# RWKV block: closing products grouped by array tile, Gram products of the two heads in turn, last doubling level in 64x64 tiles, gates on all rows

## The chip, the cores and the metric

The kernel runs on one core of a Trainium2 chip. The core has a matrix engine (PE, with a weight-load side, PEld), three engines for elementwise work (DVE, ACT, POOL), a queue engine for transfers (SP), and 16 DMA engines. The metric is the device time of one execution in microseconds; less is better. A time is the median of several runs. A profile is one further execution, recorded instruction by instruction; its times are counted from the start of its span.

## What is computed

One layer of a streaming encoder for two groups of tokens, 2048 of a prompt and 32 of a sample, with shared weights: a modulated RMSNorm, one input projection into three groups of heads (RWKV-7 time mixing, attention with forgetting, HGRN2), an output projection, then a SwiGLU network. The change is in the RWKV-7 part, which the reference writes as a scan over tokens:

```python
def rwkv7_mix(p, prev, S0, mu, w0, w2, a0, a2, g2, k_k, k_a, r_k, ln_w, ln_b):
    ...
    r, k, v, wl, al, gl = jnp.split(xs, RW_SPLITS, axis=-1)
    w_raw = -jax.nn.softplus(-(w0 + jnp.tanh(wl) @ w2)) - 0.5
    w = jnp.exp(-jnp.exp(w_raw))
    a = jax.nn.sigmoid(a0 + al @ a2)
    g = jax.nn.sigmoid(gl) @ g2
    ...
    def step(S, inp):
        r_t, k_t, v_t, kk_t, a_t, w_t = inp
        s_kk = jnp.einsum('bhvk,bhk->bhv', S, kk_t)
        S = (S * w_t[:, :, None, :] - s_kk[..., None] * (kk_t * a_t)[:, :, None, :]
             + v_t[..., None] * k_t[:, :, None, :])
        return S, jnp.einsum('bhvk,bhk->bhv', S, r_t)
    ...
    mean = jnp.mean(y, axis=-1, keepdims=True)
    var = jnp.mean(jnp.square(y - mean), axis=-1, keepdims=True)
    y = ((y - mean) * lax.rsqrt(var + RW_GN_EPS)).reshape(B, T, RW_WIDTH) * ln_w + ln_b
    bonus = jnp.sum(r * k * r_k, axis=-1, keepdims=True) * v
    y = (y + bonus.reshape(B, T, RW_WIDTH)) * g
    return y, S_T
```

There are four RWKV heads of 64 channels. The three small factors wl, al and gl have 32, 32 and 64 channels.

## The kernel before

The program first projects and recurs (`project_and_recur`), then runs attention, the output projection and the feed-forward part (`rest`). In the first part `interleave` takes turns among generators: the input projection of the next 512 tokens (lines 360 to 362, tile `ip_p`, products on the full array), the RWKV blocks, the HGRN2 blocks (tiles `hg_...`) and side work. A scheduler then orders the instructions of each engine once and for all; each engine works through its own queue in that order, with semaphores between them.

`rwkv_block` works on 128 tokens, two chunks of 64, of one pair of heads; channels of the pair lie on partitions 0 to 63 and 64 to 127 (the slices `hs`). There are 32 such blocks for the prompt and two of one chunk for the sample. Each step of a block ends in a `yield`. Its products go to one of three PSUM buffers (`rw_ps`), and ACT or DVE takes them out. The steps that matter here:

- **gates** (line 1091): three products of the low-rank factors `rl_e` (32, 32 and 64 partitions of one tile) with the weights `lw` in the same partitions. The first stands in a step of its own, the other two in one step.
- **Gram products** (line 1155): per head and chunk, `rw_kb` (lines 1143 and 1147) with `rw_G`, 64 rows by 128 columns, masked by DVE (line 1159); the second head comes a step later. POOL then scales `rw_kb` in place (line 1167), and PE transposes it (line 1170).
- **doubling**: the inverse of a unit triangular 64x64 matrix (`rw_tt`, transpose `rw_tn`), doubled from blocks of 2 to 32. Levels 2 to 16 are a loop, two products each (lines 1204 and 1213, 64x64 tiles, 32 columns moving), with an ACT copy and a masked DVE copy. The level 32 stands alone (lines 1226 and 1233), in 32x32 tiles, with two copies of 32 partitions on each engine.
- **states** (line 1268): a small chain from chunk to chunk.
- **closing products** (lines 1279 and 1280): per chunk and head two products that add up in the same 64 columns of a PSUM buffer: one with all 128 rows (128x64), one with 64 (64x64).
- **normalisation** (lines 1286 to 1300): means over the 64 channels of a head are products with constant matrices, `bmean` (ones over 64) and `rkb` (ones scaled by a weight). HGRN2 uses `bmean` too.

The closing products as they stand:

```python
        for i, h in enumerate(hs):
            nc.tensor.matmul(ps[h, cc], lhsT=wu[:, i, c, 1, :], rhs=gm[i][:, c, 64:128], start=True, stop=False)
            nc.tensor.matmul(ps[h, cc], lhsT=states[c][h, :], rhs=rp_[h, c, 0, :], start=False, stop=True)
```

## Time and profile before

| | us |
|---|---|
| median of 3 runs (3729.07 to 3733.69) | 3733.6 |
| the profiled execution | 3737.9 |
| its span, first to last instruction | 3736.2 |
| PE busy in the span | 3558.0 |
| DVE, ACT, POOL busy | 1925.2, 1501.1, 1382.6 |
| granted PE clock over the span, as a share of full speed | 0.968 |

The page counts an instruction as busy from its start to its end. Matmuls are pipelined: several are under way at once, and one that starts while the last still runs costs only the distance between the two starts. So the timeline is read from start to start. Its rows give start and length in us, engine, line, operation, output and inputs by the program's names, the part of the array (rows\*columns), the moving operand (partitions x elements), and how many instructions of a kind stand in a row. A float32 product shows as two passes, one of the projection (float32 in a rounded form) as one.

### The profile page before, as it was taken

The page shows a single profiled execution, that of the slowest core. Times are in us where ns is not written, and L with a number is a line of the kernel's source. Part 1 is how long each engine was busy: PE and PEld are TensorE (multiplying, and loading weights), DVE is VectorE, ACT ScalarE, POOL GpSimd, SP SyncE. Part 2 cuts the span into 40 slices and gives each one's busy share as a digit, 9 for nine tenths or more (in the row PEclk, how much of TensorE's full clock was granted, in tenths as well). Part 3 has the DMA queues.
Part 4 walks back from the last instruction along what each step waited for, and adds up shares of the span by engine and source line. Part 5 has one row for each costly group of instructions (what it writes and reads, how often), then busy time and mean ns, then how long its engine had stood idle before and what let it go on. Part 6 is the DMA issues. An engine that isn't in the chain of part 4 may idle for free.

```text
span 3736.2 us, 62897 instructions
## 1 busy us (share of the span) xinstructions
PE 3558.0 (95%) x24242; PEld 2969.9 (79%) x24242; DVE 1925.2 (52%) x4482; ACT 1501.1 (40%) x3526; POOL 1382.6 (37%) x1607
## 2 busy tenths in 40 slices
PE   7999999999999998899999999899999999999999
PEld 5888888888778885666666666678999998999998
DVE  3456656566565755656666655642333444333336
ACT  4355556555555645444343443331222213111212
POOL 5334444343343431644443443243233334222323
PEclk9999999999998998999999999999999999999999
DMA  6433333333542245322222213543222223111222
GB/s 216 136 103 101 83 109 120 106 95 98 177 137 73 78 122 159 121 75 74 59 77 65 81 49 75 182 137 96 68 68 74 74 71 123 59 55 56 63 62 93
DMA packets 363648, 361.38 MB, mean 97 GB/s; under 512 B 36511, under 2 KB 305396, under 8 KB 362292
## 3 DMA queue, kind: packets, MB, share of 16 engines
q1 hardware_dynamic: 325216, 320.02, 28.4%
q10 hardware_dynamic: 37748, 37.29, 3.2%
q8 instruction: 191, 3.13, 0.4%
q14 instruction: 109, 0.89, 0.1%
q0 software_dynamic: 384, 0.05, 0.0%
HBM read 291.14 MB, written 66.14 MB: 96 GB/s over the span
## 4 chain that ended last, share of the span: by engine, by line
PE 77%; DVE 6%; POOL 5%; DMA 4%; issue 4%; ACT 3%; ACTq 0%; POOLq 0%; SPq 0%; DVEq 0%
PE ff_p L1834 8%; PE ff_p L1833 8%; PE ff_p L1832 8%; PE ff_o L1783 4%; PE ff_o L1784 4%; PE ff_o L1782 4%; PE ip_p L360 4%; PE ip_p L362 4%; PE ip_p L361 4%; PE pb_pv L690 3%; PE pb_sc L643 2%; PE pb_ps L706 2%; PE pb_ps L707 1%; PE op_p L1692 1%; PE op_p L1691 1%
## 5 line engine op out<-in xcount | busy, mean ns | idle before, releaser
L1834 PE MATMUL ff_p<-h_hi,wil 128*128 128x384 f32 (+2 forms) x1760 | 623.3, 354 | 1.1 <-POOL wil L1719 1.1
L1833 PE MATMUL ff_p<-h_lo,wih 128*128 128x384 f32 (+2 forms) x1760 | 624.2, 355 | 0.1
L1832 PE MATMUL ff_p<-h_hi,wih 128*128 128x384 f32 (+2 forms) x1760 | 622.5, 354 | 1.5 <-DVE op_r L1694 0.4
L1719 POOL TENSOR_TENSOR wil<-ff_st,wih 128x1024 fp32r<-128x1024 f32 x134 | 322.2, 2404 | 582.2 <-ACT wih L1718 551.1
L360 PE MATMUL ip_p<-h_hi,w_hi 128*128 128x256 f32 (+1 forms) x1472 | 452.0, 307 | 14.0 <-ACT h_hi L296 5.9
L361 PE MATMUL ip_p<-h_lo,w_hi 128*128 128x256 f32 (+1 forms) x1472 | 436.7, 297 | 2.7 <-POOL h_lo L297 1.5
L362 PE MATMUL ip_p<-h_hi,w_lo 128*128 128x256 f32 (+1 forms) x1472 | 437.2, 297 | 0.3 <-DVE w_lo L318 0.3
L1832 PEld LDWEIGHTS ff_p<-h_hi,wih 128*128 128x128 f32 x1760 | 332.3, 189 | 17.5 <-DVE ff_sg L1763 0.8
L1834 PEld LDWEIGHTS ff_p<-h_hi,wil 128*128 128x128 f32 x1760 | 333.9, 190 | 14.4 <-POOL wil L1719 1.5
L1833 PEld LDWEIGHTS ff_p<-h_lo,wih 128*128 128x128 f32 x1760 | 332.6, 189 | 14.5 <-POOL h_lo L1907 0.6
L360 PEld LDWEIGHTS ip_p<-h_hi,w_hi 128*128 128x128 f32 x1472 | 291.4, 198 | 29.8 <-ACT h_hi L296 6.3
L1719 POOL TENSOR_TENSOR wol<-ff_st,woh 128x1024 fp32r<-128x1024 f32 x66 | 162.8, 2471 | 405.7 <-ACT woh L1718 405.6
L700 POOL TENSOR_TENSOR fx_acc<-fx_acc,fx_pt 128x512 f32<-128x512 f32 (+3 forms) x176 | 206.6, 1188 | 264.4 <-PE pb_pv L690 154.9
L1841 DVE TENSOR_TENSOR ff_sg<-ff_sg,ff_p 128x384 f32<-128x384 f32 (+2 forms) x110 | 64.5, 587 | 460.2 <-PE ff_p L1834 459.9
L361 PEld LDWEIGHTS ip_p<-h_lo,w_hi 128*128 128x128 f32 x1472 | 290.6, 197 | 9.6 <-issue 2.7
L1788 DVE TENSOR_TENSOR acc<-acc,ff_o 128x512 f32<-128x512 f32 (+1 forms) x306 | 209.1, 685 | 172.8 <-PE ff_o L1784 172.2
L1782 PE MATMUL ff_o<-woh,act_h 128*128 128x512 f32 (+1 forms) x724 | 287.9, 398 | 9.9 <-ACT act_h L1842 7.2
L362 PEld LDWEIGHTS ip_p<-h_hi,w_lo 128*128 128x128 f32 x1472 | 291.0, 198 | 7.1 <-issue 3.7
L1718 ACT ACTIVATE wih<-ff_st 128x1024 fp32r<-128x1024 f32 x134 | 142.0, 1060 | 370.6 <-PE ff_p L1833 310.5
L1783 PE MATMUL ff_o<-wol,act_h 128*128 128x512 f32 (+1 forms) x724 | 288.0, 398 | 0.0
L1784 PE MATMUL ff_o<-woh,act_l 128*128 128x512 f32 (+1 forms) x724 | 288.0, 398 | 0.0
L1718 ACT ACTIVATE woh<-ff_st 128x1024 fp32r<-128x1024 f32 x66 | 69.3, 1058 | 365.9 <-PE ff_o L1784 343.8
(466 smaller groups left out, 7718.7 us busy)
## 6 DMA issues: line engine op xcount, KB each, us to landing
ff_st<-w_ffn_in SPq DMA_DIRECT2D x132, 512.0 KB
w_st<-w_in SPq DMA_DIRECT2D x88, 512.0 KB
ff_st<-w_ffn_out SPq DMA_DIRECT2D x68, 512.0 KB
cm<-ip_e SPq DMA_DIRECT2D x92, 256.0 KB
x_t<-w_ada SPq DMA_DIRECT2D x32, 512.0 KB
fx_kr<-cm SPq DMA_DIRECT2D x80, 128.0 KB
w_st<-w_in SPq DMA_DIRECT2D x16, 520.0 KB
w_a<-w_ada SPq DMA_DIRECT2D x8, 1024.0 KB
```

Source lines behind the costliest of these rows:

```text
L360: nc.tensor.matmul(ps[:, :T], lhsT=whi[:, d, us], rhs=S.hi[:, d, :T], start=(d == 0), stop=False)
L361: nc.tensor.matmul(ps[:, :T], lhsT=whi[:, d, us], rhs=S.lo[:, d, :T], start=False, stop=False)
L362: nc.tensor.matmul(ps[:, :T], lhsT=wlo[:, d, us], rhs=S.hi[:, d, :T], start=False, stop=(d == ND - 1))
L1718: nc.scalar.activation(hi, st, AF.Copy)
L1719: nc.gpsimd.tensor_tensor(lo, st, f32(hi), ALU.subtract)
L1782: nc.tensor.matmul(ps[:m], lhsT=ah[:, js], rhs=wh[:, cs], start=(n == 0), stop=False)
L1783: nc.tensor.matmul(ps[:m], lhsT=ah[:, js], rhs=wl[:, cs], start=False, stop=False)
L1784: nc.tensor.matmul(ps[:m], lhsT=al[:, js], rhs=wh[:, cs], start=False, stop=(n == 1))
L1788: nc.vector.tensor_tensor(acc[j][:m, cs], acc[j][:m, cs], ps[:m], ALU.add)
L1832: nc.tensor.matmul(ps[:, :S], lhsT=w[0][:, ds], rhs=hh[:, d, :S], start=(d == 0), stop=False)
L1833: nc.tensor.matmul(ps[:, :S], lhsT=w[0][:, ds], rhs=hl[:, d, :S], start=False, stop=False)
L1834: nc.tensor.matmul(ps[:, :S], lhsT=w[1][:, ds], rhs=hh[:, d, :S], start=False, stop=(d == ND - 1))
```

## The change

- The closing products of a block are issued in two groups: first all 128x64 ones, then all 64x64 ones. Only the first product starts the sum, and the checks on groups are switched off.
- The Gram products of both heads are issued in one step, heads in turn, into two PSUM buffers.
- The loop of the doubling runs to 32, and the level with 32x32 tiles goes.
- `lw` gets three slices of 128 partitions with zeros outside their rows, cleared by POOL, and each gate multiplies all 128 partitions.
- `bmean` and `rkb` go; `bones` (ones) takes their place, and the factors move into the DVE or ACT instruction behind or ahead of the product.
- The states of a pair have 5 buffers instead of 6.

```diff
-    K.lw = cp.tile([128, 256], F32, name="lw")
-    nc.scalar.dma_start(out=K.lw[0:32, :], in_=a["rw_w2"][0])
-    nc.scalar.dma_start(out=K.lw[32:64, :], in_=a["rw_a2"][0])
-    nc.scalar.dma_start(out=K.lw[64:128, :], in_=a["rw_g2"][0])
+    K.lw = cp.tile([128, 3, 256], F32, name="lw")
+    nc.gpsimd.memset(K.lw, 0.0)
+    nc.scalar.dma_start(out=K.lw[0:32, 0, :], in_=a["rw_w2"][0])
+    nc.scalar.dma_start(out=K.lw[32:64, 1, :], in_=a["rw_a2"][0])
+    nc.scalar.dma_start(out=K.lw[64:128, 2, :], in_=a["rw_g2"][0])
...
-        nc.tensor.matmul(ps[:, :T], lhsT=K.lw[r0:r1, cs], rhs=lora[r0:r1, :], start=True, stop=True)
+        nc.tensor.matmul(ps[:, :T], lhsT=K.lw[:, i, cs], rhs=lora, start=True, stop=True)
...
-    gm = []
-    for h in hs:
-        ps = pt()
-        for c in range(NCH):
+    gm, gps = [], [pt() for _ in hs]
+    for c in range(NCH):
+        for ps, h in zip(gps, hs):
             nc.tensor.matmul(ps[:, 128 * c:128 * c + 128], lhsT=kb[h, c, :, :], rhs=G[h, 0:2, c, :], start=True, stop=True)
+    for ps in gps:
         v = ps[:, :128 * NCH].rearrange("p (c x) -> p c x", x=128)
...
-    for h_ in (2, 4, 8, 16):
+    for h_ in (2, 4, 8, 16, 32):
...
-        nc.vector.transpose(tn, tt)
+        if h_ < 32:
+            nc.vector.transpose(tn, tt)
         yield
-
-    ps = pt()
...
-            nc.tensor.matmul(ps[up[i], 32 * c:32 * c + 32], lhsT=m, rhs=tn[lo[i], c, 0:32], start=True, stop=True)
-    for h in up:
-        nc.scalar.activation(x[h], ps[h, :32 * NCH].rearrange("p (c x) -> p c x", x=32), AF.Copy)
-    yield
...
-            nc.tensor.matmul(ps[lo[i], 32 * c:32 * c + 32], lhsT=x[up[i], c, :], rhs=tt[up[i], c, 32:64], start=True,
-                             stop=True)
-    for h in lo:
-        nc.vector.tensor_copy(tt[h, :, 32:64], ps[h, :32 * NCH].rearrange("p (c x) -> p c x", x=32))
-    yield
...
-        s = rp.tile([128, 64], F32, name=f"rw_s{p}", bufs=6)
+        s = rp.tile([128, 64], F32, name=f"rw_s{p}", bufs=5)
...
     for c in range(NCH):
-        cc = slice(64 * c, 64 * c + 64)
         for i, h in enumerate(hs):
-            nc.tensor.matmul(ps[h, cc], lhsT=wu[:, i, c, 1, :], rhs=gm[i][:, c, 64:128], start=True, stop=False)
-            nc.tensor.matmul(ps[h, cc], lhsT=states[c][h, :], rhs=rp_[h, c, 0, :], start=False, stop=True)
+            nc.tensor.matmul(ps[h, 64 * c:64 * c + 64], lhsT=wu[:, i, c, 1, :], rhs=gm[i][:, c, 64:128], start=(c == 0),
+                             stop=False, skip_group_check=True)
+    for c in range(NCH):
+        for h in hs:
+            nc.tensor.matmul(ps[h, 64 * c:64 * c + 64], lhsT=states[c][h, :], rhs=rp_[h, c, 0, :], start=False, stop=True,
+                             skip_group_check=True)
...
-    nc.tensor.matmul(ps[:, :T], lhsT=K.bmean, rhs=y, start=True, stop=True)
-    nc.vector.tensor_tensor(y, y, ps[:, :T], ALU.subtract)
+    nc.tensor.matmul(ps[:, :T], lhsT=K.bones, rhs=y, start=True, stop=True)
+    nc.vector.scalar_tensor_tensor(y, ps[:, :T], -1.0 / 64, y, ALU.mult, ALU.add)
...
-    nc.tensor.matmul(ps[:, :T], lhsT=K.bmean, rhs=t1, start=True, stop=True)
-    nc.scalar.activation(t1, ps[:, :T], AF.Ln, bias=K.eps_c[:, 1:2])
+    nc.tensor.matmul(ps[:, :T], lhsT=K.bones, rhs=t1, start=True, stop=True)
+    nc.scalar.activation(t1, ps[:, :T], AF.Ln, bias=K.eps_c[:, 1:2], scale=1.0 / 64)
...
-    nc.vector.tensor_tensor(kp, kp, xr, ALU.mult)
+    nc.vector.scalar_tensor_tensor(kp, kp, vec(K, "rw_r_k", p), xr, ALU.mult, ALU.mult)
...
-    nc.tensor.matmul(ps[:, :T], lhsT=K.rkb[:, p, :], rhs=kp, start=True, stop=True)
+    nc.tensor.matmul(ps[:, :T], lhsT=K.bones, rhs=kp, start=True, stop=True)
```

Two places in PE's queue show how the order changes. The first is around the Gram products of a block in the middle of the projection; each row gives line, operation, output and inputs, and size. `ip_p` is the projection, L1300 the last normalisation product of an older block, L1226 the first half of the last doubling level. Before:

```order
L1155 MATMUL rw_ps<-rw_G,rw_kb 128x128 x2
L1300 MATMUL rw_ps<-rw_a,rkb 128x128
L1226 MATMUL rw_ps<-rw_tn,rw_m_12340 32x32
L1226 MATMUL rw_ps<-rw_tn,rw_gm_12362 32x32
L1226 MATMUL rw_ps<-rw_tn,rw_m_12340 32x32
L1226 MATMUL rw_ps<-rw_tn,rw_gm_12362 32x32
L361 MATMUL ip_p<-h_lo,w_hi 128x256
L362 MATMUL ip_p<-h_hi,w_lo 128x256
L360 MATMUL ip_p<-h_hi,w_hi 128x256
L361 MATMUL ip_p<-h_lo,w_hi 128x256
L1155 MATMUL rw_ps<-rw_G,rw_kb 128x128 x2
L362 MATMUL ip_p<-h_hi,w_lo 128x256
```

After (L1151, L1280 and L1201 are the changed kernel's lines for L1155, L1300 and the doubling's first product):

```order
L1151 MATMUL rw_ps<-rw_G,rw_kb 128x128 x4
L1280 MATMUL rw_ps<-rw_a,bones 128x128
L362 MATMUL ip_p<-h_hi,w_lo 128x256
L360 MATMUL ip_p<-h_hi,w_hi 128x256
L361 MATMUL ip_p<-h_lo,w_hi 128x256
L362 MATMUL ip_p<-h_hi,w_lo 128x256
L1201 MATMUL rw_ps<-rw_tn,rw_m_12303 64x32
L1201 MATMUL rw_ps<-rw_tn,rw_gm_12322 64x32
L1201 MATMUL rw_ps<-rw_tn,rw_m_12303 64x32
L1201 MATMUL rw_ps<-rw_tn,rw_gm_12322 64x32
```

The second head's Gram products move up beside the first's, so PE visits their form once; the last doubling level has the lines and sizes of the levels before it and stands four projection passes later.

The second place is the closing products of a block, also in PE's queue; `rw_gm_...` with `rw_wu` are the 128x64 products of the two heads, `rw_rp` with `rw_s_...` the 64x64 ones. Before:

```order
L362 MATMUL ip_p<-h_hi,w_lo 128x256
L1279 MATMUL rw_ps<-rw_gm_12338,rw_wu 64x64
L1280 MATMUL rw_ps<-rw_rp,rw_s_12161 64x64
L1279 MATMUL rw_ps<-rw_gm_12362,rw_wu 64x64
L1280 MATMUL rw_ps<-rw_rp,rw_s_12161 64x64
L1279 MATMUL rw_ps<-rw_gm_12338,rw_wu 64x64
L1280 MATMUL rw_ps<-rw_rp,rw_s_13052 64x64
L1279 MATMUL rw_ps<-rw_gm_12362,rw_wu 64x64
L1280 MATMUL rw_ps<-rw_rp,rw_s_13052 64x64
L1213 MATMUL rw_ps<-rw_tt,rw_x_1460 64x32 x4
```

After, at the same place (L1255 and L1259 are the two groups, L1210 the doubling's second product):

```order
L362 MATMUL ip_p<-h_hi,w_lo 128x256
L1255 MATMUL rw_ps<-rw_gm_12301,rw_wu 64x64
L1255 MATMUL rw_ps<-rw_gm_12322,rw_wu 64x64
L1255 MATMUL rw_ps<-rw_gm_12301,rw_wu 64x64
L1255 MATMUL rw_ps<-rw_gm_12322,rw_wu 64x64
L1259 MATMUL rw_ps<-rw_rp,rw_s_12121 64x64 x2
L1259 MATMUL rw_ps<-rw_rp,rw_s_13008 64x64 x2
L1210 MATMUL rw_ps<-rw_tt,rw_x_1456 64x32 x4
```

The products are the same and stand between the same neighbours; only their order among themselves changes, from eight changes of form to one.

## Prediction

> **What bounds the kernel now.** I read the stretches of the span first, then the waits of the matrix engine (PE) in the one stretch that the change touches, then its timeline there.

> ```profile
> PE 3558.0 (95%) x24242; PEld 2969.9 (79%) x24242; DVE 1925.2 (52%) x4482; ACT 1501.1 (40%) x3526; POOL 1382.6 (37%) x1607
> 0.00:163.00 163.00, 131.35 (x972) 118.75 (x973) 60.86 (x155) 65.63 (x116) 74.52 (x186) 0.96 0.55 182
> 163.00:1361.00 1198.00, 1156.26 (x11686) 986.33 (x11685) 725.86 (x2459) 681.83 (x2154) 463.31 (x896) 0.95 0.36 107
> 1361.00:2460.00 1099.00, 1010.03 (x5167) 713.67 (x5166) 655.98 (x1243) 474.04 (x838) 445.15 (x324) 0.96 0.33 95
> ```

> The first row gives busy time of the engines over the whole span; the others give, for a stretch, its length, then busy time and instructions of PE, PEld (weight loads), DVE, ACT and POOL, the granted clock, the share of the DMA engines and GB/s. I cut the span so that the second stretch, 163 to 1361 us, holds all matrix products of the RWKV blocks. There PE is busy for 1156 of 1198 us, 97%, while DVE has 61%, ACT 57%, POOL 39% and the DMA engines 36%. The stretch is as long as PE needs for the instructions in its queue, plus 42 us of waiting. From the last closing product on, the order of instructions is the same in both kernels on all five engines, so what lies behind only starts earlier. The question is how much PE time goes, and how much of that comes back as waiting.

> ```profile
> PE rw_ps L1155 <- DVE rw_kb L1147: 9.9, 8, 2.6
> PE rw_ps L1170 <- POOL rw_kb L1167: 8.2, 8, 2.4
> PE rw_ps L1204 <- DVE rw_tn L1216: 3.5, 4, 1.1
> ```

> These are the three longest of PE's waits in the stretch (us in total, times, longest one): short ones, each behind a chain of small DVE, ACT or POOL instructions.

> **The change, part by part.** A float32 product shows as two passes, so "x8" below is four products. The form (64\*64, 128\*64, ...) is the part of the array used, rows by columns. What counts is start to start, since the ends overlap. There are 32 prompt blocks (16 pieces of 128 tokens, 2 head pairs) and 2 sample blocks of half the size.

> *Closing products.*

> ```profile
> 604.05 0.33 PE L1279 MATMUL rw_ps<-rw_gm,rw_wu 128*64 128x64 f32 x2
> 604.30 0.32 PE L1280 MATMUL rw_ps<-rw_rp,rw_s 64*64 64x64 f32 x2
> ...
> 606.10 0.39 PE L391 MATMUL ip_p<-w_hi,h_lo 128*128 128x260 f32 x1
> 917.07 0.45 PE L1261 MATMUL rw_ps<-rw_wu,rw_gm 128*64 128x64 f32 x8
> 917.46 0.24 PE L1204 MATMUL rw_ps<-rw_tn,rw_m 64*64 64x32 f32 x1
> 668.47 0.45 PE L1194 MATMUL rw_ps<-rw_wu,rw_gm 64*64 64x64 f32 x8
> 668.85 0.38 PE L361 MATMUL ip_p<-h_lo,w_hi 128*128 128x256 f32 x1
> ```

> Before, the eight products of a block alternate between two forms, and each costs 0.25 us, 2.05 us in all. Afterwards four of form 128\*64 come first, then four of 64\*64. L1261 is the first group exactly (same form, same sizes, heads in turn) and takes 0.39 us; L1194 is the second and takes 0.38 us. So 2.05 - 0.77 = 1.28 us go per block, 41 us for 32; a sample block has half as many, some 0.6 us each. **41 us**, bounds 39 and 43.

> [...]

> *Gram products.*

> ```profile
> 614.97 0.71 PE L1155 MATMUL rw_ps<-rw_G,rw_kb 64*128 64x128 f32 x4
> 615.61 0.49 PE L1300 MATMUL rw_ps<-rw_a,rkb 128*128 128x128 f32 x2
> 498.86 0.48 PE L1155 MATMUL rw_ps<-rw_G,rw_kb 64*128 64x128 f32 x2
> 499.27 0.49 PE L1300 MATMUL rw_ps<-rw_a,rkb 128*128 128x128 f32 x2
> 671.40 0.65 PE L1244 MATMUL rw_ps<-rw_kn,rw_tt 64*64 64x128 f32 x8
> 671.89 0.19 PE L1204 MATMUL rw_ps<-rw_tn,rw_m 64*64 64x32 f32 x1
> ```

> A head's visit to the form 64\*128 takes 0.64 us with four passes and 0.41 with two: 0.115 us a pass and 0.18 for coming and going. Now both heads come in one visit of eight passes, alternating between the upper and the lower rows. No row shows two such tiles at once. If the passes don't overlap, the visit takes 0.18 + 8 x 0.115 = 1.10 and 0.18 us is saved; if pairs run together, it takes 0.64 and 0.64 is saved. L1244 is the nearest: 64\*64 tiles of both heads with the same 128 columns moving, eight passes in 0.49, which only fits pairs. I take pairs: 32 x 0.64 = 20 us, and 2 us for fewer changes from and to the full array (next rows). **22 us**, bounds 8 and 24.

> *Gates.*

> ```profile
> 638.32 0.28 PE L362 MATMUL ip_p<-h_hi,w_lo 128*128 128x256 f32 x1
> 638.44 0.28 PE L360 MATMUL ip_p<-h_hi,w_hi 128*128 128x256 f32 x1
> 638.65 0.42 PE L1213 MATMUL rw_ps<-rw_tt,rw_x 64*64 64x32 f32 x8
> 639.00 0.39 PE L361 MATMUL ip_p<-h_lo,w_hi 128*128 128x256 f32 x1
> 918.17 0.48 PE L1091 MATMUL rw_ps<-rl_e,lw 32*128 32x128 f32 x2
> 918.59 0.33 PE L1268 MATMUL rw_ps<-rw_s,rw_rp 64*64 64x64 f32 x4
> 601.20 0.90 PE L1091 MATMUL rw_ps<-rl_e,lw 32*128 32x128 f32 x4
> 602.03 0.49 PE L1439 MATMUL hg_ps<-hg_x,hg_k 64*64 64x160 f32 x4
> 423.85 0.39 PE L1128 MATMUL rw_ps<-rw_kk,bones 128*128 128x128 f32 x2
> 424.07 0.39 PE L1286 MATMUL rw_ps<-rw_y,bmean 128*128 128x128 f32 x2
> 424.38 0.24 PE L1204 MATMUL rw_ps<-rw_tn,rw_m 64*64 64x32 f32 x1
> ```

> A pass of the projection (L362 to L360) costs 0.12 us, the step from it to another form 0.21. A block's first gate costs 0.42 us, the other two together 0.83. With all rows a gate has the form of L1128, which comes from and goes to the full array in 0.22, and L1286 leaves it in 0.31. Among full-array work the pair falls from 0.83 to 0.53, the single gate from 0.42 to between 0.22 and 0.31, and 0.09 goes at each entry. Between two small forms the change of form is still paid and little is saved. In the order about half of the visits begin beside full-array work: 34 x about 0.38 = **13 us**, bounds 0 (all between small forms) and 24.

> *Last level.*

> ```profile
> 621.04 0.31 PE L1233 MATMUL rw_ps<-rw_tt,rw_x 32*32 32x32 f32 x8
> 621.28 0.39 PE L360 MATMUL ip_p<-h_hi,w_hi 128*128 128x256 f32 x1
> ```

> In 32\*32 tiles a half of the level takes 0.24 us; in 64\*64, as L1213 above, 0.35. Twice 0.11 for 33 blocks' worth is 7 us lost; where the neighbours are 64\*64 too, the changes of form go and nothing is lost. **6 us lost**, bounds 0 and 7. Two half-height copies become one on ACT (L1228) and on DVE (L1236), which lie beside PE's work; without that cover they would be worth some 0.2 us each per block.

> ```profile
> L1228 ACT ACTIVATE rw_x<-rw_ps 32x64 f32<-32x64 f32 x64 | 13.8, 215 | 38.5 <-PE rw_ps L1226 34.2 <-PE rw_ps L1155 1.5 <-POOL rw_y L1304 1.4
> L1236 DVE COPY rw_tt<-rw_ps 32x64 f32<-32x64 f32 x64 | 13.6, 213 | 11.4 <-PE rw_ps L1233 10.6
> 0.96 0.31 POOL L80 MEMSET sc<- 128x256 f32 x1
> 30.64 1.06 ACT L316 ACTIVATE w_hi<-w_st 128x1024 fp32r<-128x1024 f32 x1 [5.92 <-DMA w_st<-w_in]
> ```

> *The rest.* The means by one matrix of ones instead of two scaled ones keep the number and the sizes of the products; the DVE and ACT instructions take a scale and keep their sizes. The new clearing of the gate weights on POOL is three times the memset of L80, 0.9 us as an estimate, ahead of three DMA issues in ACT's queue. ACT sits idle for 5.92 us soon after, until the weights land, which hides it; without that it costs 0.9 us once. Five state buffers instead of six: a block needs three at a time, and the next one brings two, so none is waited for. All of this: 0.

> **Sum.** PE work: -41 - 22 - 13 + 6 = -70 us, 6% of the 1156; by the bounds -39 - 8 - 0 + 7 = -40 and -43 - 24 - 24 + 0 = -91. Not all comes through. The chains behind the 42 us of waits keep their length while the PE work that covers them gets 6% shorter, and chains that just fitted now show. In return POOL's step L1167 may begin once both heads' Gram products are done, which now happens in one visit, so its 8.2 us should shrink. I put the net at 14 us given back, 20% of the 70: **-56 us**. The profiled execution took 3737.9 us (span 3736.2 and 1.7 around it), 0.1% over the median 3733.6; 3737.9 - 56 = 3682 there, **3678** by the median.

> **Rivals.**
> - *The Gram tiles don't pair.* 14 us less PE work, 45 us net: 3689. For it: no row shows two 64\*128 tiles at once. Against: L1244. Chance 0.13.
> - *Waits swallow more.* The block is a long chain, and PE's order is fixed; if half of the 70 returns as waits: 3699, with three quarters 3716. For it: waits on single DVE and POOL instructions of up to 2.6 us. Against: 97% busy. Chance 0.13.
> - *More comes through.* The wait for POOL goes, gates and Gram reach their upper bounds: -80, 3654. Chance 0.14.
> - [...] Chance 0.04.
> - *Slower: the Gram visit takes two of the three PSUM buffers of the block at once*, so both heads wait until two are free and the next product until DVE has masked one. DVE is 61% busy, and the longest wait here was 2.6 us. From 1.7 us per visit on (56 / 33) the gain is gone; at 2.6 us it would be 86 us and the time 3764. Against: the places of the visits in PE's queue hardly move. Chance 0.04.

> **How the numbers follow.** My forecast of 3678, between 3664 and 3690, has 0.52. The range runs from 3650 to 3710: it leaves out the rival that is slower, the far end of the waits and of the upper bounds. 0.2%, 7.5 us, is about what a measurement of this kernel tells from no change. All cases but one end faster by more; with something for a mix of small gains and new waits: faster 0.92, same 0.04, slower 0.04.

> **What would show it.** In the profile of the changed kernel the four products of the first closing group should take 0.39 us and the second 0.38; eight Gram passes 0.64 (1.10 if unpaired); a gate among full-array work 0.22 to 0.31; PE busy in the RWKV stretch about 1085 us, the waits 50 to 60 us, the stretch some 1142 us long, and the stretches behind it as before. I am wrong if the stretch shortens by less than 30 us, or if PE's busy time falls by 70 us and the stretch does not follow.

## The result, and the profile after

| | kernel before | kernel after |
|---|---|---|
| median of the runs | 3731.3 us (3727.5 to 3733.7, 4 runs) | 3646.6 us (3640.3 to 3650.6, 4 runs) |
| ratio, with its 95% interval | | 0.9772 (0.9755 to 0.979) |
| profiled execution | 3737.9 us | 3650.6 us |
| PE busy in the RWKV stretch | 1156 of 1198 us | 1054 of 1111 us |
| waits of PE there | 42 us | 57 us |

The change made the kernel 85 us faster. 56 were forecast, and 3647 lies just outside the range from 3650 to 3710. The next fence has the engines' row of the page after; the second one two stretches, with the columns as above.

```profile
PE 3454.1 (95%) x24242; PEld 2893.4 (79%) x24242; DVE 1917.3 (53%) x4445; ACT 1486.8 (41%) x3492; POOL 1376.2 (38%) x1608
```

```profile
163.00:1274.00 1111.00, 1054.07 (x11709) 914.95 (x11709) 717.62 (x2426) 669.10 (x2124) 460.72 (x900) 0.98 0.39 116
1274.00:2373.00 1099.00, 1009.29 (x5164) 712.82 (x5162) 654.94 (x1242) 473.81 (x838) 444.36 (x324) 0.96 0.33 95
```

Over the whole span PE is busy for 104 us less (3454 against 3558). The first stretch ends where the last RWKV product ends, 87 us earlier than before. The second is 1099 us long, as before. So the whole gain lies in the RWKV stretch, as forecast. PE is busy for 102 us less there, where 70 were forecast, and waits 15 us longer. The granted clock in the row is 0.98; before it was 0.95.

The timeline of PE shows the new groups (start, length, line, form, passes; "..." leaves out what stands between).

```profile
572.22 0.49 PE L1088 MATMUL rw_ps<-rl_e,lw 128*128 128x128 f32 x2
572.46 0.37 PE L389 MATMUL ip_p<-w_hi,h_hi 128*128 128x260 f32 x1
...
576.52 0.61 PE L1088 MATMUL rw_ps<-rl_e,lw 128*128 128x128 f32 x4
577.06 0.62 PE L1419 MATMUL hg_ps<-hg_x,hg_k 64*64 64x160 f32 x6
...
578.87 0.28 PE L390 MATMUL ip_p<-w_lo,h_hi 128*128 128x260 f32 x1
579.08 0.45 PE L1255 MATMUL rw_ps<-rw_gm,rw_wu 128*64 128x64 f32 x8
579.46 0.45 PE L1259 MATMUL rw_ps<-rw_rp,rw_s 64*64 64x64 f32 x8
579.84 0.39 PE L391 MATMUL ip_p<-w_hi,h_lo 128*128 128x260 f32 x1
...
589.17 0.72 PE L1151 MATMUL rw_ps<-rw_G,rw_kb 64*128 64x128 f32 x8
589.82 0.54 PE L1419 MATMUL hg_ps<-hg_x 64*64 64x96 f32 x6
```

Start to start, the closing groups take 0.38 and 0.38 us (0.39 and 0.38 forecast, 2.05 before); with the entry from the product ahead, eight changes of form have become two, not one. Eight Gram passes take 0.65 us (0.64 forecast; 1.10 if the tiles did not pair). Here a single gate takes 0.24 (0.22 to 0.31 forecast among full-array work; over all single visits the median is 0.32) and a pair 0.54 (0.53). The prices in the prediction came out. The waits of PE in the stretch, the longest five:

```profile
PE rw_ps L1210 <- ACT rw_x L1205: 9.6, 16, 1.5
PE rw_ps L1201 <- DVE rw_tn L1214: 8.9, 13, 1.1
PE rw_ps L1151 <- DVE rw_kb L1144: 7.3, 6, 2.3
PE rw_ps L1221 <- DVE rw_tt L993: 4.4, 4, 2.4
PE rw_ps L1229 <- ACT rw_wu L1224: 4.3, 4, 3.2
```

The wait for POOL's L1167 (8.2 us before) is gone. In its place the two products of a doubling level (L1201, L1210) wait for the DVE and ACT steps between them: the chains that just fitted now show.

**Where the other 30 us are.** The granted clock has two values in the traces of both kernels, 1.00 and 0.50, here called full and half. Before, 123 us of the stretch ran at half clock, after 44 us (the mean of 0.95 over 1198 us says the same: 2 x 0.05 x 1198 = 120). PE's time therefore has three parts. I put every step from one pass to the next at the mean that steps between the same two shapes have at full clock: their sum is the *work*. What the steps during half clock took beyond that is *lost to half clock*. The rest, in which PE stands idle, is *waits*. For the first pair of profiles this gives work 1103 to 1034 us, lost to half clock 53 to 19, waits 42 to 57: -68 - 34 + 15 = -87. The terms of the prediction, -70 and +14, came out near; it had no term for the clock.

### The profile page after: what moved, and what is told of

The parts are those of the page before. It is cut to its first block, busy times and chain, and to the rows that moved or that the text cites. A ratio compares the mean times of both kernels' runs of the same rounds, so it can differ in the third digit from the quotient of the medians.

```text
span 3648.6 us, 62814 instructions
## 1 busy us (share of the span) xinstructions
PE 3454.1 (95%) x24242; PEld 2893.4 (79%) x24242; DVE 1917.3 (53%) x4445; ACT 1486.8 (41%) x3492; POOL 1376.2 (38%) x1608
## 4 chain that ended last, share of the span: by engine, by line
PE 72%; DVE 7%; POOL 6%; ACT 6%; DMA 5%; issue 4%; ACTq 0%; SPq 0%; POOLq 0%; DVEq 0%
PE ff_p L1814 8%; PE ff_p L1813 8%; PE ff_p L1812 8%; PE ff_o L1764 4%; PE ff_o L1763 4%; PE ff_o L1762 4%; PE pb_pv L690 4%; PE ip_p L360 3%; PE ip_p L361 3%; PE ip_p L362 3%; PE pb_sc L643 2%; PE pb_ps L706 2%; PE op_p L1672 1%; PE op_p L1671 1%; PE op_p L1670 1%
## 5 line engine op out<-in xcount | busy, mean ns | idle before, releaser
L360 PE MATMUL ip_p<-h_hi,w_hi 128*128 128x256 f32 (+1 forms) x1472 | 442.2, 301 | 14.2 <-ACT h_hi L296 5.4
L361 PE MATMUL ip_p<-h_lo,w_hi 128*128 128x256 f32 (+1 forms) x1472 | 429.6, 292 | 4.1 <-POOL h_lo L297 1.9
L362 PE MATMUL ip_p<-h_hi,w_lo 128*128 128x256 f32 (+1 forms) x1472 | 428.3, 291 | 0.3 <-DVE w_lo L318 0.3
L360 PEld LDWEIGHTS ip_p<-h_hi,w_hi 128*128 128x128 f32 x1472 | 283.6, 193 | 27.5 <-ACT h_hi L296 6.0
L361 PEld LDWEIGHTS ip_p<-h_lo,w_hi 128*128 128x128 f32 x1472 | 283.5, 193 | 10.8 <-issue 2.7
L362 PEld LDWEIGHTS ip_p<-h_hi,w_lo 128*128 128x128 f32 x1472 | 283.3, 193 | 7.6 <-issue 5.4
L318 POOL TENSOR_TENSOR w_lo<-w_st,w_hi 128x256 fp32r<-128x256 f32 (+2 forms) x220 | 160.7, 760 | 153.1 <-ACT w_hi L316 125.3
```

The lines of the kernel that those rows point to most:

```text
L360: nc.tensor.matmul(ps[:, :T], lhsT=whi[:, d, us], rhs=S.hi[:, d, :T], start=(d == 0), stop=False)
L361: nc.tensor.matmul(ps[:, :T], lhsT=whi[:, d, us], rhs=S.lo[:, d, :T], start=False, stop=False)
L362: nc.tensor.matmul(ps[:, :T], lhsT=wlo[:, d, us], rhs=S.hi[:, d, :T], start=False, stop=(d == ND - 1))
```

## The experiments

The questions were whether the clock's part is real or the luck of one profile, which part of the change brings what, and why the clock is granted more often. "Half clock" is the time in the stretch at half clock, "forms" the changes of form from one pass to the next. Times in us. The ratio is the one on record with its interval; it can differ a little from that of the two medians.

| kernel | median | ratio to before on the same chip | work | waits | lost | half clock | forms |
|---|---|---|---|---|---|---|---|
| before, first profile | 3731.3 | | 1103 | 42 | 53 | 123 | 1459 |
| before, again | 3710.6 (one run) | | 1105 | 40 | 38 | 89 | 1459 |
| closing alone | 3674.0 | 0.9876 (0.9854 to 0.9899) | 1069 | 44 | 30 | 72 | 1277 |
| Gram alone | 3712.4 | 0.9981 (0.9954 to 1.0008) | 1092 | 45 | 39 | 92 | 1448 |
| gates alone | 3702.6 | 0.9943 (0.9927 to 0.996) | 1090 | 46 | 28 | 68 | 1365 |
| last level alone | 3726.1 | 1.0004 (0.999 to 1.0018) | 1108 | 39 | 45 | 106 | 1432 |
| after, first profile | 3646.6 | 0.9772 (0.9755 to 0.979) | 1034 | 57 | 19 | 44 | 1107 |
| after, again | 3642.4 | 0.9789 (0.9758 to 0.982) | 1031 | 57 | 21 | 48 | 1107 |
| after, closing undone | 3674.9 | 0.9873 (0.9845 to 0.9901) | 1073 | 50 | 28 | 65 | 1302 |
| after, Gram undone | 3676.8 | 0.988 (0.9854 to 0.9905) | 1057 | 52 | 32 | 75 | 1149 |
| after, gates undone | 3654.4 | 0.9824 (0.9794 to 0.9855) | 1048 | 49 | 23 | 55 | 1199 |
| after, last level undone | 3646.5 | 0.98 (0.9772 to 0.9828) | 1036 | 51 | 23 | 55 | 1158 |
| after, filler on 128 rows | 3679.1 | 0.9894 (0.9869 to 0.9919) | 1080 | 46 | 14 | 34 | 1118 |
| the same, again | 3682.4 | 0.989 (0.9857 to 0.9923) | 1080 | 48 | 15 | 38 | 1118 |
| after, filler on 32 rows | 3692.5 | 0.9929 (0.9903 to 0.9956) | 1081 | 45 | 22 | 51 | 1130 |
| after, gates in one visit | 3640.6 | 0.9783 (0.9751 to 0.9815) | 1029 | 60 | 17 | 41 | 1070 |

**Each part alone, on the kernel before.** Four kernels take over one part of the diff each.

*Closing:*

```diff
-            nc.tensor.matmul(ps[h, cc], lhsT=wu[:, i, c, 1, :], rhs=gm[i][:, c, 64:128], start=True, stop=False)
-            nc.tensor.matmul(ps[h, cc], lhsT=states[c][h, :], rhs=rp_[h, c, 0, :], start=False, stop=True)
+            nc.tensor.matmul(ps[h, 64 * c:64 * c + 64], lhsT=wu[:, i, c, 1, :], rhs=gm[i][:, c, 64:128], start=(c == 0),
+                             stop=False, skip_group_check=True)
+    for c in range(NCH):
+        for h in hs:
+            nc.tensor.matmul(ps[h, 64 * c:64 * c + 64], lhsT=states[c][h, :], rhs=rp_[h, c, 0, :], start=False, stop=True,
+                             skip_group_check=True)
...
```

> The kernel before with the closing products grouped, and nothing else. The full change gained 85 us by the medians where the terms gave 56; in its profile the RWKV stretch has 102 us less PE busy time and 15 us more waiting, and the time at half the clock in the stretch fell from 123 to 44 us, which is about 39 us of work. Theory 'density': each change of form leaves the array without moving columns for a while, so the clock is granted less often; parts that remove changes of form also remove time at half clock. Closing alone then: 41 us of work, some 20 us of clock, 10 us given back: about 50 us faster, 3680 to 3685, half-clock time in the stretch 70 to 95 us. Rival 'waits': half-clock time follows the long waits for DVE and POOL, which this part does not touch: it stays at 110 to 135 us, 41 us of work less 8 of waits, some 33 us faster, 3698.

46 us faster by the ratio (1 - 0.9876 of 3725), 51 by the medians. The work fell by 35 us, the half-clock time to 72. That is what "density" expected, though one profile each can't tell it from chance.

*Gram:*

```diff
-    for h in hs:
-        ps = pt()
-        for c in range(NCH):
+    gm, gps = [], [pt() for _ in hs]
+    for c in range(NCH):
+        for ps, h in zip(gps, hs):
...
```

> The kernel before with the Gram products of the two heads in turn, and nothing else. By the terms: 22 us of PE work. Density: with some 8 us of clock and 5 us given back, about 25 us faster, 3706, half-clock time 95 to 115 us. Waits: this part moves the waits for POOL (8.2 us) away and they were what slowed the clock: the half-clock time falls most here, by 40 us or more, and it is 40 us faster, 3690.

7 us faster by the ratio, with no change inside its interval: both expectations missed. The groups of PE by shape show that the pairs run together here too. First the kernel before, then Gram alone (passes | busy us, mean ns of one | idle us ahead):

```profile
L1155 PE MATMUL rw_ps<-rw_G,rw_kb 64*128 64x128 f32 x264 | 49.5, 309 | 10.0 <-DVE rw_kb L1147 9.9
```

```profile
L1154 PE MATMUL rw_ps<-rw_G,rw_kb 64*128 64x128 f32 x264 | 27.6, 308 | 8.5 <-DVE rw_kb L1147 8.4
```

The group's own time falls by 22 us, but the work of the stretch by 12 only. What is lost seems to lie in the order: 34 visits fewer, yet only 11 changes of form fewer (1459 to 1448), and those to and from the full array rise from 964 to 976.

*Gates, with the one matrix of ones and five state buffers (they make room):*

```diff
-        nc.tensor.matmul(ps[:, :T], lhsT=K.lw[r0:r1, cs], rhs=lora[r0:r1, :], start=True, stop=True)
+        nc.tensor.matmul(ps[:, :T], lhsT=K.lw[:, i, cs], rhs=lora, start=True, stop=True)
```

> The kernel before with the gates on all rows, the one matrix of ones and five state buffers (the edits that need or free the space), and nothing else. By the terms 13 us of PE work (0 to 24). Density: two gates in a block no longer change the form where they stand among full-array work: 13 us and some 5 us of clock, 3 us given back, 15 us faster, 3716. Waits: 10 us faster at most, half-clock time unchanged, 3721 to 3731.

21 us faster. The work fell by 14 us, as the term of 13 said; the half-clock time fell to 68 us, further than "density" said.

*Last level:*

```diff
-    for h_ in (2, 4, 8, 16):
+    for h_ in (2, 4, 8, 16, 32):
...
-            m = (mt[0][:32] if i == 0 else gm[1][64:96])[:, c, 32:64]
-            nc.tensor.matmul(ps[up[i], 32 * c:32 * c + 32], lhsT=m, rhs=tn[lo[i], c, 0:32], start=True, stop=True)
```

> The kernel before with the last doubling level in the loop, in 64x64 tiles, and nothing else. By the terms 6 us of PE work more (0 to 7) and two DVE and ACT copies fewer: 0 to 6 us slower, 3731 to 3737. Density: 64x64 products follow others of that form, so changes of form go and a little clock comes back: 0 to 5 us faster. This run also shows how far the half-clock time of the stretch (123 us before) moves from one profile to another where little is changed: within 20 us if it is a property of the order, more if it is chance.

No difference in time; 4 us more work, as the term of 6 said, and 2 us less waiting.

By the ratios the four add up to 46 + 7 + 21 - 1.5 = 73 us, by the medians to 51 + 13 + 23 - 1 = 85; so the times alone don't tell whether the parts simply add.

**Is the clock's part real?** The kernel before and the kernel after were profiled again, the latter timed on another chip.

> The kernel before, unchanged, for a second profile of it. In the first the stretch has 123 us at half clock and loses 53 us by it; the last level alone, which changes little, showed 106 and 45. If the half-clock time is a property of the order: 100 to 125 us here, and 20 to 45 us for the full change whenever it is profiled. If it is chance from run to run: anything from 45 to 150.

> The full change, unchanged, timed against the kernel before on another chip, with a second profile. The two profiles of the kernel before have 123 and 89 us of the stretch at half clock and lose 53 and 38 us by it, at the same work (1103 and 1105 us) and waits (42 and 40); so a single profile says little about the clock. Work and waits alone make the change 68 + 2 - 15 = 53 to 55 us faster. If the clock term is real: again 80 to 90 us faster (0.976 to 0.979), half-clock time 30 to 60 us here. If it was chance of the few executions: 55 to 70 us faster (0.981 to 0.985), half-clock time 60 to 110 us.

The stretch of the kernel before, and then of the kernel after, in these second profiles:

```profile
163.00:1346.00 1183.00, 1142.99 (x11692) 975.85 (x11691) 725.70 (x2460) 681.61 (x2155) 463.50 (x898) 0.96 0.36 109
```

```profile
163.00:1272.00 1109.00, 1052.43 (x11684) 912.52 (x11683) 716.81 (x2425) 666.76 (x2121) 459.72 (x897) 0.98 0.38 116
```

Work and waits return within 4 us; the loss to half clock does so after the change (19 and 21 us) but not before it (53 and 38; the half-clock time of 89 us lies below the 100 to 125 of a fixed property of the order). On average of two profiles the loss is 45 us before and 20 after. With the means of both pairs: work 1104 to 1033, -71; waits 41 to 57, +16; clock 45 to 20, -25; together -80. The two measured ratios give -85 and -79.

Two profiles of a kernel are few, but each timed execution has its granted clock on record, over the whole span. With two values of the clock, the time at half clock is 2 x (1 - clock) x time. In 37 executions of the kernel before, on four chips (clock 0.968 to 0.977), that is 207 us on average, with a standard deviation of 17; in eight of the kernel after, on two (0.976 to 0.982), it is 159 us. So the change takes away 47 us at half clock, and the clock's part is real. Among executions of the kernel before on the same chip, 1 us more at half clock goes with 0.38 us more time (correlation 0.95). By that the 47 us are worth 18 us, by the 53 of 123 in the first profile 20. The 25 above is too much, because the first profile of the kernel before (0.968, 241 us over its whole span) was one of the worst. Work, waits and a clock part of 18 to 20 make -73 to -75; what is missing to -79 and -85 stays open.

**Each part undone, on the kernel after.** The first three, and the last level below, are the pieces of the diff backwards; the gates come with their scaled matrices of ones and six state buffers.

```diff
-    for c in range(NCH):
-        for i, h in enumerate(hs):
-            nc.tensor.matmul(ps[h, 64 * c:64 * c + 64], lhsT=wu[:, i, c, 1, :], rhs=gm[i][:, c, 64:128], start=(c == 0),
...
+            nc.tensor.matmul(ps[h, cc], lhsT=wu[:, i, c, 1, :], rhs=gm[i][:, c, 64:128], start=True, stop=False)
+            nc.tensor.matmul(ps[h, cc], lhsT=states[c][h, :], rhs=rp_[h, c, 0, :], start=False, stop=True)
```

> The full change with the closing products alternating again, all else kept. Counted with every step from pass to pass at its mean at full clock, the full change took 68 us of work out of the stretch and 34 us of time lost to half clock, and added 15 us of waits; closing alone took out 34 of work and 23 of clock. Density: 34 us of work and some 15 to 20 us of clock come back, less 5 of waits: 45 us above the full change, about 3692 (0.990 of before), half-clock time in the stretch 70 to 100 us. Chance: the work comes back, the clock stays: 3675 to 3680, half-clock time 35 to 55 us.

40 us of work come back, 7 us of waits go, and 8 us are lost to half clock; the ratio rises by 0.0084 to 0.0101, 31 to 38 us. "Density" asked for a ratio of 0.990, "chance" for 0.985 to 0.986: the interval holds both. By the profile's half-clock time (65 us) neither range does. By the clock of its four executions the kernel has 164 us at half clock over the whole span, the full change 159: hardly any clock comes back, which speaks for "chance". (A mean of four executions is uncertain by some 8 us, half of the 17.)

```diff
-    gm, gps = [], [pt() for _ in hs]
-    for c in range(NCH):
-        for ps, h in zip(gps, hs):
+    gm = []
+    for h in hs:
+        ps = pt()
+        for c in range(NCH):
...
```

> The full change with the Gram products head after head again, all else kept. Alone the Gram part took out 11 us of work (22 forecast) although its visits show the pairs; the four parts alone add up to 52 us of work, the full change to 68. If the missing 11 us belong to the order that the scheduler makes around the merged visit, and the other parts repair it, then undoing it here costs 22 to 27 us of work: 3670 to 3680. If the parts simply add, it costs 11 us of work, 3655 to 3662.

24 us of work come back: the forecast term of 22, and twice what the part made alone. In this order the changes of form do go: from here to the full change 42 fewer (1149 to 1107), 14 of them to and from the full array. So Gram's missing 10 us were lost to the order and not to the tiles. The parts don't add: alone they make 57 us of work (35 + 12 + 14 - 4), undone 82 (40 + 24 + 15 + 3), and the full change has 71.

```diff
-        nc.tensor.matmul(ps[:, :T], lhsT=K.lw[:, i, cs], rhs=lora, start=True, stop=True)
+        nc.tensor.matmul(ps[:, :T], lhsT=K.lw[r0:r1, cs], rhs=lora[r0:r1, :], start=True, stop=True)
```

> The full change with the gates on 32, 32 and 64 rows again (and so with the scaled matrices of ones and six state buffers), all else kept. Alone the gates made 21 us (13 forecast): 13 us of work and the rest in the clock. If the parts add: 13 us of work come back and 15 to 20 us of time, less 3 of waits. If the gates save less in the new order than alone, because more of their visits begin beside small forms: 5 to 8 us of work.

15 us of work come back, as alone, and 13 us of time against the full change on the same chip (0.9824 to 0.9789), though the two intervals overlap. By the clock of the executions 19 us at half clock come back too (174 against 155 on this chip); alone the gates took away 20 (213 to 193). It is the one part whose clock shows both ways: closing alone took away 29 (213 to 184) but, undone, brings nearly none back; Gram alone took none (222), though with it undone 191 us run at half clock.

```diff
-    for h_ in (2, 4, 8, 16, 32):
+    for h_ in (2, 4, 8, 16):
...
+    for c in range(NCH):
+        for i in range(2):
+            m = (mt[0][:32] if i == 0 else gm[1][64:96])[:, c, 32:64]
...
```

> The full change with the last doubling level in 32x32 tiles again, all else kept. Alone this part added 5 us of work (6 forecast) and took 3 us of waits away, 0 in the time. If the parts add: 5 us less work than the full change, 3 to 5 us more waits, time within 5 us of it. If the forms count as in the grouping (32x32 between 64x64 products are extra changes): 5 to 10 us slower. If the term of 6 comes through: 6 us faster than the full change, and the fastest kernel so far.

4 us slower than the full change by the medians, which the runs can't tell from none. Undone, the level costs 3 us more work, where on the kernel before its 64x64 tiles cost 4 more. Two profiles of one kernel differ by 3 as well (1034 and 1031), so this is no more than a hint that the level now stands among its like. Undoing a part lowers the waits by 5 to 8 us in each of the four kernels; that fits waits left uncovered as the work shrinks, which belong to no single part.

**What stands ahead of half clock.** In the first profiles of both kernels every half-clock stretch begins a whole multiple of 3.41 us behind the one before it (43 stretches before, 29 after, over the whole span), and those in the RWKV stretch last 3.41 to 20.48 us. So I cut the time into windows of 3.41 us at these beginnings; "the grid" below means these cuts. Ahead of half clock, PE can be busy for the whole window, though more often it waits. A window and the half-clock stretch behind it, in the first profile of the kernel before:

```profile
1276.36:1279.77 3.41, 3.41 (x32) 2.50 (x28) 2.56 (x10) 2.56 (x8) 3.27 (x8) 1.00 0.13 35
1279.77:1286.60 6.83, 6.83 (x43) 5.83 (x44) 2.97 (x10) 2.28 (x9) 3.03 (x9) 0.50 0.00 0
```

PE is busy for 3.41 of 3.41 us, then the clock is 0.50 for 6.83 us, whose row counts 43 passes; the 3.41 us before have 32. The timeline shows what PE was busy with:

```profile
1276.81 0.90 PE L1091 MATMUL rw_ps<-rl_e,lw 32*128 32x128 f32 x4
1277.64 0.33 PE L1268 MATMUL rw_ps<-rw_s,rw_rp 64*64 64x64 f32 x4
1277.90 0.39 PE L389 MATMUL ip_p<-w_hi,h_hi 128*128 128x260 f32 x1
...
1278.46 0.24 PE L1204 MATMUL rw_ps<-rw_tn,rw_m 64*64 64x32 f32 x1
...
1279.13 0.33 PE L1279 MATMUL rw_ps<-rw_gm,rw_wu 128*64 128x64 f32 x2
1279.39 0.32 PE L1280 MATMUL rw_ps<-rw_rp,rw_s 64*64 64x64 f32 x2
```

Small products with a change of form between them. The page of the profile counts them as busy, but columns move for only 47% of this window (an estimate, counted as said below).

It isn't the usual case. Of the 196 half-clock stretches that begin in the RWKV stretches of the 16 profiles, 35 follow a window in which PE was busy for at least 90% of the time, and 137 one with less than 70%; only one of these windows was idle throughout. One in which PE waits, in the kernel before, and the one behind it:

```profile
501.54:504.95 3.41, 1.24 (x10) 0.79 (x8) 3.12 (x10) 0.00 (x0) 3.33 (x9) 1.00 0.14 39
504.95:508.36 3.41, 3.20 (x15) 3.18 (x16) 1.31 (x7) 2.59 (x10) 0.85 (x4) 0.50 0.89 254
```

PE is busy for 1.24 of 3.41 us. The two profiles of the kernel before have 7 and 3 half-clock stretches behind windows with PE busy for at least 90%, and 13 and 13 behind the others; after the change there are 0 and 1, and 7 and 7. So nearly all of the first kind go with the change, and half of the second, although PE waits longer in all. So half clock followed windows in which PE waits as well, and more often (137 against 35 of the 196).

To test density at an equal price, three more products a block, on the full array, went in where the alternation had cost its 1.3 us.

```diff
+    for _ in range(3):
+        nc.tensor.matmul(ps[:, 128:384], lhsT=K.bones, rhs=K.reset, start=True, stop=True)
     for c in range(NCH):
         for i, h in enumerate(hs):
             nc.tensor.matmul(ps[h, 64 * c:64 * c + 64], lhsT=wu[:, i, c, 1, :], rhs=gm[i][:, c, 64:128], start=(c == 0),
...
```

> The full change with work of the same price as the alternating closing products put in their place, but dense: three extra products a block on the full array (bones with a constant tile of 256 columns, into unused columns of the closing buffer, read by nobody), ahead of the grouped closing products. At two passes of 256 columns (0.43 us a product by L360's 0.12 us a pass of 256 columns at half that width's rate, doubled) this adds 1.3 us for each of 33 blocks: 42 us of work. Density: columns move all the time in it, so the clock does not suffer: half-clock time 25 to 45 us, some of the 57 us of waits is covered, 30 to 40 us above the full change, 3677 to 3687, and clearly less half-clock time than with the closing undone. Chance: half-clock time as in the run with the closing undone, whatever it is there, and the two kernels end within 8 us of each other.

Work +47 us, half-clock time 34 us; with the closing undone, work +40 and 65 us. The half-clock times of the profiles are those of "density", but the two medians are 4 us apart, and by the clock of the executions the two kernels have 160 and 164 us at half clock over the whole span: that is what "chance" said. Alternating closing products in the place of dense ones took hardly any clock away here (164 against 160 us). To see what stands ahead of half clock, I counted windows instead of kernels: all 5072 windows of the grid in the RWKV stretches of the 16 profiles that began at full clock, by the share in which columns move (an estimate: 0.107 us for 128 columns of a float32 product, the least distance between L195's passes of 128 columns, and half of that in the projection, whose passes of 256 columns follow every 0.12 us) and by whether a product on 32 rows (a gate of 32 rows, a 32x32 tile) stands in them; and how many were followed by half clock.

| share of the window in which columns move | no product on 32 rows | with one |
|---|---|---|
| under 40% | 102 of 115 | 22 of 23 |
| 40 to 50% | 39 of 223 | 26 of 47 |
| 50 to 60% | 0 of 489 | 5 of 133 |
| over 60% | 0 of 3501 | 2 of 541 |

Density tells most: half clock followed 124 of the 138 windows under 40%, and 7 of the 4664 over 50%. (In the first profiles of both kernels PE was busy for at most 70% of each of the 19 windows under 40%.) It doesn't tell all: between 40 and 50% half clock followed about 60% of the windows with PE busy for over 99%, and about 20% of the others. And at the same share half clock followed windows with products on 32 rows more often: 26 of 47 against 39 of 223 between 40 and 50%, 5 of 133 against 0 of 489 between 50 and 60%. The last kernel tests the rows by themselves: the filler on 32 rows in place of 128, with the same columns in the same order.

```diff
-        nc.tensor.matmul(ps[:, 128:384], lhsT=K.bones, rhs=K.reset, start=True, stop=True)
+        nc.tensor.matmul(ps[:, 128:384], lhsT=K.bones[0:32, :], rhs=K.reset[0:32, :], start=True, stop=True)
```

> The kernel with the filler on the full array, unchanged, beside the one on 32 rows on the same chip: 33 us above the full change as before (0.989 of the kernel before), half-clock time 30 to 45 us by both theories.

> The kernel with the filler, its three extra products a block now on 32 rows (the first 32 partitions of the same two constant tiles) in place of 128, with the same columns and the same order; read by nobody. What the thirteen profiles show so far: in a window of 3.41 us without products on 32 rows, half clock follows in 26 of 60 cases if columns move in 45 to 50% of it, and in 1 of 3194 above 55%; with such products in it, half clock follows in 15 of 72 cases between 55 and 65%. Theory 'rows': products on 32 rows count for less than the time in which their columns move; the filler of 1.3 to 1.5 us on 32 rows then lets its windows fall under the bound: half-clock time in the stretch 70 to 200 us in place of 34, and the time 10 to 60 us above that with the full filler. Theory 'columns': only the time in which columns move counts: half-clock time 30 to 60 us, the time within 10 us of the full filler, save for two more changes of form a block (some 7 us).

(In that text the projection's passes count at the float32 pace too, which puts its shares some tenth higher than the table's.) Half-clock time 51 us in place of 34 and 38, lost 22 in place of 14 and 15, the time 10 us more by the medians, with intervals that overlap. That is less than "rows" asked for, and inside the range of "columns". But two of its ten half-clock stretches follow windows in which columns moved for 65 and 69%; both hold the filler on 32 rows. No other of the 196 follows a window above 55%. One of them, and its timeline:

```profile
1141.00:1144.41 3.41, 3.41 (x35) 2.52 (x35) 0.65 (x2) 3.28 (x16) 0.78 (x2) 1.00 0.54 156
1144.41:1147.82 3.41, 3.41 (x17) 3.41 (x18) 1.74 (x5) 1.91 (x6) 0.51 (x1) 0.50 0.13 43
```

```profile
1141.98 1.56 PE L1254 MATMUL rw_ps<-reset,bones 32*128 32x256 f32 x6
1143.47 0.45 PE L1257 MATMUL rw_ps<-rw_gm,rw_wu 128*64 128x64 f32 x8
1143.85 0.45 PE L1261 MATMUL rw_ps<-rw_rp,rw_s 64*64 64x64 f32 x8
```

The same filler on 128 rows, six passes in the same 1.5 us, in the profile again:

```profile
621.62 1.56 PE L1254 MATMUL rw_ps<-reset,bones 128*128 128x256 f32 x6
623.11 0.45 PE L1257 MATMUL rw_ps<-rw_gm,rw_wu 128*64 128x64 f32 x8
```

The profiled execution was the fastest of the five, at the highest clock (0.978). Over all five the mean clock is 0.975, against 0.979 in the four of the filler on 128 rows on the same chip: 185 against 156 us at half clock over the whole span. At 0.38 us each the 29 us are worth 11, which is the 10 between the medians, at the same work within 1 us. So the filler on 32 rows had more half clock here. The effect was smaller than "rows" asked for. I take it that this is because columns move for at least 64% of all 43 windows that hold this filler: over 60%, half clock followed 2 of 4042 windows.

**A version beyond the change.** The three gates of a block side by side in one PSUM buffer, in one visit.

```diff
+    gp = pt()
+    for i in range(3):
+        nc.tensor.matmul(gp[:, T * i:T * i + T], lhsT=K.lw[:, i, cs], rhs=lora, start=True, stop=True)
...
-        ps = pt()
-        nc.tensor.matmul(ps[:, :T], lhsT=K.lw[:, i, cs], rhs=lora, start=True, stop=True)
+        ps = gp[:, T * i:T * i + T]
...
```

> The full change with the three gate products of a block side by side in one PSUM buffer and in one visit, ahead of the first gate's DVE and ACT steps; nothing else is moved. One visit of two passes less for 33 blocks; beside full-array work that saves about 0.2 us each, beside small forms 0.1: 3 to 7 us of work. The waits may grow by 2 to 3 us since the buffer is held longer. If the work comes through: 3 to 6 us faster than the full change (0.976 to 0.978 of before); if the waits eat it, the same.

4 us less work, 3 us more waits: 0.9783 (0.9751 to 0.9815), the same as the full change. In the profile the waits ate most of the saving; a gain of 3 to 6 us would be too small for these runs to show.

## Why the prediction fell short

- **What bounds the kernel** was right: PE in the RWKV stretch, and nothing behind it moved.
- **Closing, -41:** 35 us of work alone, 40 when undone. The first group takes 0.38 us in the trace, where 0.39 was forecast.
- **Gram, -22:** 24 us when undone, but 12 alone. The tiles pair: eight passes take 0.65 us. The 2 us for fewer changes to and from the full array depend on the order: their count rises by 12 with Gram alone, falls by 14 with Gram in the full change, and stays in the whole change (964 and 962).
- **Gates, -13:** 14 us alone, 15 undone. **Last level, +6:** 4 alone, -3 in the full change.
- **Work in all, -70:** -71. **Given back as waits, +14:** +16; the 20% behind it was chosen and not worked out from rows, so its coming out is partly luck. The wait for POOL went, as said.
- **The step that failed** is the sum itself: it was made of durations at full clock and put a change of the clock at nothing, without a reason, although 53 of the 1156 us of busy time were lost to half clock. The windows' row quoted in the prediction has the clock, 0.95, and the prediction made nothing of it. In its place the runs showed 47 us less at half clock, worth 18 to 20 us (25 by the means of two profiles). The rival "more comes through" named nearly the right time (3654), mostly for another reason: it put the gates and Gram at their upper bounds of 24 us each, where the gates made 14 or 15 and Gram 12 to 24, and it had no clock either.

What stays open is why the clock is granted more often. By the counts in the table above, and averaged over all positions of the grid, I estimate that about 15 half-clock stretches should begin in the RWKV stretch before the change and 10 after it, nearly all of the difference, by this estimate, from the windows that no longer hold products on 32 rows; the share of windows under 40% hardly changes. The profiles had 20 and 16 before, 7 and 8 after. At some 6 us of half clock for each, of which 43% are lost (53 of 123), that makes 13 of the 18 to 20 us. The 19 us at half clock that come back with the gates undone, and the 29 of the filler on 32 rows, point the same way. Where the rest comes from, these runs don't tell. A kernel that changes the rows of the gates alone, with their changes of form kept, was not tried.

## What to carry to other kernels

In this kernel small products cost twice: by the pause at each change of form (the eight closing products of a block took 2.05 us alternating and 0.76 in two groups), and by the half clock that began behind windows in which PE was busy for at least 90% (7 and 3 stretches in the two profiles before, 0 and 1 after). So group products of one form into one visit, and give them full rows where the zeros are free (the gates: 14 us of work). Read the granted clock of the stretch beside PE's busy share before pricing a change there, and put its loss into the sum as a term of its own. Take the clock from many executions and not from one profile (two profiles of the kernel before had 123 and 89 us at half clock). A part that is measured alone may show half its worth, if the order around it changes (Gram: 12 us of work alone, 24 undone).
